# A chunked state-space scan kept in PSUM with one scan per tile, and a softmax whose rows are scaled on ScalarE

## The chip, the cores and the metric

The kernel runs on one core of one Trainium2 chip. The metric is the device time of one execution in microseconds (us). A profiled execution gives a trace of every engine: PE is the matrix engine (TensorE), DVE is VectorE, ACT is ScalarE, POOL is GpSimd, and SP is the engine whose queue issues the DMAs.

## The reference

Two layers (DEPTH = 2) of a gated mixer on x with 512 rows and width 1024, all in float32. Cut to what matters:

```
proj  = x @ w_in[l]         # u, z_ssm, c_q, c_kv, k_rope, z_mla, q_mem, z_mem, gate logits
y_ssm = S5(u)               # diagonal complex recurrence h[t] = lam * h[t-1] + B u[t];  y = Re(C h) + d * u
y_ssm = GLU(gelu(y_ssm)) * silu(z_ssm)
y_mla = causal attention, 8 heads, scores scaled by 96 ** -0.5, softmax over the row
y_mem = attention into 256 memory rows, 4 heads, scores scaled by 128 ** -0.5, softmax
x     = LayerNorm(ALPHA * x + (sum of gate * (branch @ p_branch)) @ w_out)
```

The S5 branch works on 512 features in 32 groups of 16, with 64 states a group. `gelu` is the tanh form.

## The kernel before

Every large matmul is three products of float32r parts (`mm3`, L72; lines 75, 76 and 77 in the trace), so an operand has to be split into a high part (a cast, mostly on ACT: L551, with a factor L554) and a low part (a subtraction, mostly on DVE: L552, with a factor L555) before PE can use it. `E.clk` counts the matmul time that the program has issued so far, in us of full-rate matmuls.

**Order of the work.** PE runs its instructions in the order in which the program writes them. The other engines and SP's DMA queue get an order from a scheduler, and each then works through its own list in that order: a waiting instruction holds up all that stand behind it on its engine. One layer is: the latents, then the memory keys (layer 0) and the memory attention (`mem_phase`), then one merge, two z tiles (`zs=2`), the GLU tiles (`glu_tile`, which reads the four entries of `E.g` in turn for k = 0 to 3), the latent attention (`mla_phase`) and the output.

**The S5 branch** is a background stream, `s5_stream` (L523). `tick` lets it go one stage on whenever `E.clk` has reached the value that the stream gave last. So its matmuls stand between those of the memory attention and the merge, at distances that a table of delays (`CFG`, L1282) gives in matmul time. A layer has four u tiles; `s5_tile` (L432) does one, of eight groups, in these stages:

- U is loaded (L443); `kp`: 16 small matmuls (L451, L452), copied to `kt` on ACT (L454), two small DVE operations (L458) and two DMAs to `kd` (L459);
- `tp`: two times four transposes (L465), each copied to `bmT` on ACT (L466);
- `tz` is loaded back from `kd` (L469); the next tile's operators are started on GpSimd (`s5_pool`, L358);
- `pb`: eight matmuls of 64 columns (L475), and then on DVE the chain L478 to L493: rotate (four operations), eight scans of 64 columns (L485), rotate back (four) into `z`;
- `py`: matmuls with `tz` and `U`, then with `t.cl` and `z` (L500); GELU on ACT and DVE (L501 to L505);
- `yt`: transposes (L509), a copy `y` on ACT (L511), a DMA out (`yd`, L513) and back (`yb`, L515), and the split of `yb` (L519, which calls `split_to`: L554 on ACT, L555 on DVE) into `E.g`.

`kp`, `tp`, `pb`, `py` and `yt` share one PSUM buffer (`s5=1`), so each can start only when the one before it has been read.

The softmax (`softmax_ops`, L713) takes the row maximum on DVE (L716), multiplies it by -scale on DVE (L717), takes exp on ACT (L718), inverts the sum on DVE (L719) and scales the row on DVE (L720); `mem_scores` calls it 32 times in the two layers and `mla_scores` 64 times.

Of the kernel before, what the change touches and what calls it, by code (L numbers as in the profile page):

```python
# [256 lines left out]
def param_setup(E):  # L257
    """The small S5 parameters of both layers."""
# [50 lines left out]
def rope_tables(E):  # L309
    """Cosines and signed sines of the rope angles, features on partitions."""  # L310
# [26 lines left out]
def s5_powers(E, l):  # L337
    """Powers of the discrete poles of one layer, then those of their phases."""
# [19 lines left out]
def s5_pool(E, l, ut):  # L358
    """Chunk operators of the eight groups of one u tile, as far as GpSimd builds them."""
# [61 lines left out]
def u_tile(E, l, ut):  # L421
    """One tile of u^T, regrouped through DRAM for the chunked scan."""
# [9 lines left out]
def s5_tile(E, l, ut, t):  # L432
    """Chunked scan of eight groups; leaves the split GELU of the SSM output in E.g.

    Yields how much matmul time should pass before its next stage."""
# [41 lines left out]
    a, b = mid("ra"), mid("rb")  # L477
# [69 lines left out]
def split_to(E, hi, lo, src, scale=1.0, eng=None):  # L547
    """hi + lo = scale * src, both float32r."""
# [22 lines left out]
def wblock(E, src, n=512, eng=None):  # L571
    """One [128, n] float32 block of weights as two float32r parts."""
# [26 lines left out]
def w_in_tile(E, l, t, eng=None):  # L599
    """One 128-column tile of x @ w_in, transposed, in PSUM."""  # L600
# [10 lines left out]
def warm_up(E):  # L611
    """Matmuls of zeros that open the tensor engine's clock gate while the first loads are under way."""
# [7 lines left out]
def first_tiles(E, l):  # L620
    """The latent tiles side by side, as x arrives."""
# [44 lines left out]
def gate2(E, ps):  # L666
    """2 * silu of a PSUM tile."""
# [7 lines left out]
def mem_load(E, tags):  # L675
    """mem^T, two feature tiles per block."""
# [61 lines left out]
def mem_values_out(E, l, h, Ps, z, fill):  # L738
    """Attention output of one memory head times its SiLU gate (twice)."""
# [19 lines left out]
def latents(E, l):  # L759
    """RMS-normalised q and kv latents (two parts each) and the rotated shared key."""  # L760
# [53 lines left out]
def scale_latents(E, l, cs, rs):  # L814
    """Norms and gains applied to the latents."""
# [12 lines left out]
def rotary_sums(E):  # L828
    """The partial sums of the shared key added up, as they are and with swapped halves."""
# [5 lines left out]
def rotate_key(E, ps):  # L835
    """The rotated shared key, two parts."""
# [9 lines left out]
def mla_v(E, l, i):  # L846
    """Values of four heads, two key tiles to a tile."""
# [13 lines left out]
def mla_k(E, l, hp):  # L861
    """Keys of two heads, with the rotated part."""
# [16 lines left out]
def mla_q(E, l, hp, j, wq):  # L879
    """Rotated queries of one head."""  # L880
# [11 lines left out]
    split_to(E, q[0][0:96, :], q[1][0:96, :], qf[0:96, :])  # L892
# [4 lines left out]
def mla_scores(E, q, k, Ps):  # L897
    """Softmax rows of one head, by query tiles."""
# [528 lines left out]
```

## Time and profile before

| | |
|---|---|
| three runs | 1161.16, 1162.88 (median), 1163.74 us |
| profiled execution | span 1161.9 us from the first to the last instruction, mean granted PE clock 0.965 |
| busy PE, DVE, ACT, POOL | 1075.1 (93%), 781.0 (67%), 456.9 (39%), 486.9 (42%) us |
| chain that ended last | PE 64%, DVE 20%, DMA 8% |

The profiled execution's own time lies in its span and the little around it, which no row shows; the median of the runs is 1.0 us above the span. A busy share of an engine is an average over the whole span. What an engine waited for is found in the table of waits, and where PE ran slowly in the tables by window, whose column PEclk is the granted clock as a share of full speed.

### The profile page before, as it was taken

The page shows a single profiled execution, that of the slowest core. Times are in us where ns is not written, and L with a number is a line of the kernel's source. Part 1 is how long each engine was busy: PE and PEld are TensorE (multiplying, and loading weights), DVE is VectorE, ACT ScalarE, POOL GpSimd, SP SyncE. Part 2 cuts the span into 40 slices and gives each one's busy share as a digit, 9 for nine tenths or more (in the row PEclk, how much of TensorE's full clock was granted, in tenths as well). Part 3 has the DMA queues.
Part 4 walks back from the last instruction along what each step waited for, and adds up shares of the span by engine and source line. Part 5 has one row for each costly group of instructions (what it writes and reads, how often), then busy time and mean ns, then how long its engine had stood idle before and what let it go on. Part 6 is the DMA issues. An engine that isn't in the chain of part 4 may idle for free.

```text
span 1161.9 us, 15913 instructions
## 1 busy us (share of the span) xinstructions
PE 1075.1 (93%) x5584; PEld 862.6 (74%) x5584; DVE 781.0 (67%) x1522; ACT 456.9 (39%) x906; POOL 486.9 (42%) x577
## 2 busy tenths in 40 slices
PE   9859897799999999999989979879999999999995
PEld 6658775677877777788868767667888777778885
DVE  7696969747687784753585796695547767644428
ACT  5314342233554443333334334323335544433331
POOL 3997854762023243763540365481000333320163
PEclk9969998999999999999989989989999999999998
DMA  6423242445222222444544424334332222234341
GB/s 212 146 65 122 55 114 69 108 106 126 89 80 66 67 64 66 135 127 128 155 133 139 116 64 114 76 85 118 104 100 82 71 66 65 73 110 126 102 144 73
DMA packets 87664, 117.96 MB, mean 102 GB/s; under 512 B 24096, under 2 KB 36512, under 8 KB 87584
## 3 DMA queue, kind: packets, MB, share of 16 engines
q1 hardware_dynamic: 86944, 114.85, 34.7%
q0 software_dynamic: 640, 2.10, 0.7%
q8 instruction: 44, 0.72, 0.3%
q14 instruction: 36, 0.29, 0.1%
HBM read 107.37 MB, written 9.55 MB: 101 GB/s over the span
## 4 chain that ended last, share of the span: by engine, by line
PE 64%; DVE 20%; DMA 8%; issue 4%; ACT 3%; POOL 1%; SPq 0%; DVEq 0%; ACTq 0%; POOLq 0%
PE mm L75 17%; PE mm L77 17%; PE mm L76 17%; DVE w L552 4%; PE av L929 2%; DVE rb L485 2%; DMA yb<-yd 2%; DMA raw<-in_w_mem_kv 2%; PE tp L921 2%; DMA yd<-ra 2%; PE py L500 1%; PE pb L475 1%; DVE P L720 1%; DVE hl L552 1%; DVE mx L716 1%
## 5 line engine op out<-in xcount | busy, mean ns | idle before, releaser
L75 PE MATMUL mm<-X,w 128*128 128x512 f32 x740 | 300.2, 406 | 0.2 <-ACT X L551 0.2
L77 PE MATMUL mm<-X,w 128*128 128x512 f32 x740 | 290.8, 393 | 0.0
L76 PE MATMUL mm<-X,w 128*128 128x512 f32 x740 | 290.1, 392 | 0.2 <-DVE X L552 0.2
L552 DVE TENSOR_TENSOR w<-raw,w 128x512 fp32r<-128x512 f32 (+2 forms) x247 | 211.8, 862 | 114.9 <-ACT w L551 113.9
L551 ACT CAST w<-raw 128x512 fp32r<-128x512 f32 (+1 forms) x317 | 191.9, 607 | 206.7 <-PE mm L77 71.9
L552 POOL TENSOR_TENSOR w<-raw,w 128x512 fp32r<-128x512 f32 x70 | 92.8, 1328 | 307.8 <-ACT w L551 123.5
L75 PEld LDWEIGHTS mm<-X,w 128*128 128x128 f32 x740 | 141.1, 191 | 30.6 <-issue 3.2
L77 PEld LDWEIGHTS mm<-X,w 128*128 128x128 f32 x740 | 139.6, 189 | 31.4 <-DVE w L552 0.8
L76 PEld LDWEIGHTS mm<-X,w 128*128 128x128 f32 x740 | 140.6, 190 | 26.7 <-DVE X L552 0.7
L77 PE MATMUL mm<-hl,w 128*128 128x512 f32 (+1 forms) x296 | 111.3, 376 | 15.5 <-DVE w L552 15.5
L75 PE MATMUL mm<-hl,w 128*128 128x512 f32 (+1 forms) x296 | 113.1, 382 | 0.0
L76 PE MATMUL mm<-hl,w 128*128 128x512 f32 (+1 forms) x296 | 110.6, 374 | 0.0
L77 PEld LDWEIGHTS mm<-hl,w 128*128 128x128 f32 x296 | 58.0, 196 | 25.8 <-DVE w L552 16.4
L75 PEld LDWEIGHTS mm<-hl,w 128*128 128x128 f32 x296 | 58.3, 197 | 8.9 <-issue 0.5
L76 PEld LDWEIGHTS mm<-hl,w 128*128 128x128 f32 x296 | 58.1, 196 | 8.6
L987 ACT ACTIVATE thg<-mm,bg 128x512 f32<-128x512 f32 x48 | 32.9, 686 | 63.3 <-PE mm L77 63.3
L872 POOL TENSOR_SCALAR hl<-hl 32x512 fp32r<-32x512 f32 x32 | 22.5, 702 | 74.1 <-PE mm L76 54.0
L718 ACT ACTIVATE P<-sa,mx 128x128 f32<-128x128 f32 (+1 forms) x64 | 33.8, 528 | 47.4 <-DVE mx L717 47.4
L998 POOL TENSOR_TENSOR macc<-macc,thg 128x512 f32<-128x512 f32 x16 | 24.4, 1526 | 65.3 <-DVE thg L997 61.6
L720 DVE TENSOR_SCALAR P<-P,mx 128x256 f32<-128x256 f32 (+2 forms) x96 | 47.3, 493 | 2.6
L997 DVE SCALAR_TENSOR_TENSOR thg<-thg,mm 128x512 f32<-128x512 f32 x32 | 22.0, 687 | 39.3 <-PE mm L77 39.2
L375 POOL MEMSET bt<- 128x16 f32 x8 | 0.9, 110 | 109.9 <-PE kp L452 109.9
(386 smaller groups left out, 2047.3 us busy)
## 6 DMA issues: line engine op xcount, KB each, us to landing
raw<-in_w_in SPq DMA_DIRECT2D x188, 256.0 KB
raw<-in_p SPq DMA_DIRECT2D x48, 256.0 KB
raw<-in_w_mem_kv SPq DMA_DIRECT2D x32, 256.0 KB
raw<-in_w_out SPq DMA_DIRECT2D x32, 256.0 KB
tz<-kd SPq DMA_DIRECT2D x8, 512.0 KB
raw<-in_w_glu SPq DMA_DIRECT2D x16, 256.0 KB
raw<-in_xT SPq DMA_DIRECT2D x8, 256.0 KB
raw<-in_memT SPq DMA_DIRECT2D x8, 256.0 KB
```

What stands on the lines that cost most here:

```text
L75: t.matmul(out, lhsT=a[0], rhs=b[0], start=start, stop=False)
L76: t.matmul(out, lhsT=a[0], rhs=b[1], start=False, stop=False)
L77: t.matmul(out, lhsT=a[1], rhs=b[0], start=False, stop=stop)
L485: v.tensor_tensor_scan(out=b[:, o], data0=E.r8[:, gi:gi + 1].to_broadcast([128, 64]), data1=a[:, o], initial=0.0, op0=ALU.mult, op1=ALU.add)
L551: nc.scalar.copy(hi, src)
L552: (eng or nc.vector).tensor_tensor(out=lo, in0=src, in1=fl(hi), op=ALU.subtract)
L718: nc.scalar.activation(out=P, in_=ps, func=AF.Exp, bias=mx[:, 1:2], scale=scale, accum_out=mx[:, 2:3])
L720: nc.vector.tensor_scalar(out=P, in0=P, scalar1=mx[:, 3:4], scalar2=None, op0=ALU.mult)
L921: nc.tensor.transpose(tp[:, cols(t)], Ps[t][:, cols(kb)], E.ident)
L929: mm = lambda out, rhs, start, stop: nc.tensor.matmul(out, lhsT=w, rhs=rhs, start=start, stop=stop)
L987: nc.scalar.activation(out=th, in_=pg, func=AF.Tanh, bias=E.bg2[:, col:col + 1], scale=0.5)
L998: (v if last else nc.gpsimd).tensor_tensor(out=E.macc[m], in0=E.macc[m], in1=th, op=ALU.add)
```

## The change

In the S5 tile the rotated input, the scanned values and the rotation back stay in `pb`, in PSUM; only the cross terms go to SBUF (`b`). One scan of 512 columns replaces eight of 64: its factors come from a new tile `r8`, which holds each group's pole radius 63 times behind a zero, so that the scan starts anew at each group. `r8` is filled by an ACT copy and a small memset. GELU loses one DVE operation, its factors going into the two ACT operations. The split of `yb` becomes a function `tail`, which runs in the next tile's `kp` stage (for the last tile after `tok_us`). The delays change. In the softmax the score scale goes into the split of the queries, the maximum comes out negated, and the row is scaled on ACT.

```diff
-def s5_tile(E, l, ut, t):
+def s5_tile(E, l, ut, t, tail):
...
-    yield 1.3
+    if tail is not None:
+        tail()
+    yield E.cfg["kt_us"]
...
-        yield 1.3 if h == 0 else E.cfg["pb_us"]
+        yield E.cfg["pb_us"]
...
+    r8 = mid("r8")
+    gi = l * NG + ut * 8
+    v.memset(g3(r8, 0, 1), 0.0)
+    nc.scalar.copy(g3(r8, 1, 63), E.r8[:, gi:gi + 8].rearrange("p (g o) -> p g o", o=1).to_broadcast([128, 8, 63]))
     pb = ptile("pb")
...
-    v.tensor_tensor(out=a, in0=pb, in1=t.cos, op=ALU.mult)
-    v.tensor_tensor(out=b[0:64, :], in0=pb[64:128, :], in1=t.sin[64:128, :], op=ALU.mult)
-    v.tensor_tensor(out=b[64:128, :], in0=pb[0:64, :], in1=t.sin[0:64, :], op=ALU.mult)
-    v.tensor_tensor(out=a, in0=a, in1=b, op=ALU.add)
-    for q in range(8):
-        o = slice(q * 64, q * 64 + 64)
-        gi = l * NG + ut * 8 + q
-        v.tensor_tensor_scan(out=b[:, o], data0=E.r8[:, gi:gi + 1].to_broadcast([128, 64]), data1=a[:, o], initial=0.0,
-                             op0=ALU.mult, op1=ALU.add)
...
-    v.tensor_tensor(out=g3(z, 1), in0=g3(b), in1=g3(t.cos), op=ALU.mult)
-    v.tensor_tensor(out=a[0:64, :], in0=b[64:128, :], in1=t.sin[64:128, :], op=ALU.mult)
-    v.tensor_tensor(out=a[64:128, :], in0=b[0:64, :], in1=t.sin[0:64, :], op=ALU.mult)
-    v.tensor_tensor(out=g3(z, 1), in0=g3(z, 1), in1=g3(a), op=ALU.subtract)
+    def swapped():
+        v.tensor_tensor(out=b[0:64, :], in0=pb[64:128, :], in1=t.sin[64:128, :], op=ALU.mult)
+        v.tensor_tensor(out=b[64:128, :], in0=pb[0:64, :], in1=t.sin[0:64, :], op=ALU.mult)
+
+    swapped()
+    v.tensor_tensor(out=pb, in0=pb, in1=t.cos, op=ALU.mult)
+    v.tensor_tensor(out=pb, in0=pb, in1=b, op=ALU.add)
+    v.tensor_tensor_scan(out=pb, data0=r8, data1=pb, initial=0.0, op0=ALU.mult, op1=ALU.add)
+    swapped()
+    v.tensor_tensor(out=pb, in0=pb, in1=t.cos, op=ALU.mult)
+    v.tensor_tensor(out=g3(z, 1, 63), in0=g3(pb, 0, 63), in1=g3(b, 0, 63), op=ALU.subtract)
...
-    nc.scalar.activation(out=a, in_=py, func=AF.Square)
-    v.tensor_scalar(out=a, in0=a, scalar1=0.044715, scalar2=1.0, op0=ALU.mult, op1=ALU.add)
-    v.scalar_tensor_tensor(out=a, in0=a, scalar=GELU_C, in1=py, op0=ALU.mult, op1=ALU.mult)
-    nc.scalar.activation(out=a, in_=a, func=AF.Tanh)
+    nc.scalar.activation(out=a, in_=py, func=AF.Square, scale=math.sqrt(0.044715))
+    v.scalar_tensor_tensor(out=a, in0=a, scalar=1.0, in1=py, op0=ALU.add, op1=ALU.mult)
+    nc.scalar.activation(out=a, in_=a, func=AF.Tanh, scale=GELU_C)
...
-    yield E.cfg["tok_us"]
-    h, lo = ftile2(E, "A")
-    w = lambda i: i.rearrange("p (n j) -> p j n", j=8)
-    split_to(E, w(h), w(lo), yb.rearrange("p (j n) -> p j n", j=8), 0.5)
-    E.g.append(HL(h, lo))
+
+    def tail():
+        h, lo = ftile2(E, "A")
...
+    return tail
...
-    nc.vector.reduce_max(out=mx[:, 0:1], in_=ps, axis=AX.X)
-    nc.vector.tensor_scalar(out=mx[:, 1:2], in0=mx[:, 0:1], scalar1=-scale, scalar2=None, op0=ALU.mult)
-    nc.scalar.activation(out=P, in_=ps, func=AF.Exp, bias=mx[:, 1:2], scale=scale, accum_out=mx[:, 2:3])
+    nc.vector.reduce_max(out=mx[:, 1:2], in_=ps, axis=AX.X, negate=True)
+    nc.scalar.activation(out=P, in_=ps, func=AF.Exp, bias=mx[:, 1:2], accum_out=mx[:, 2:3])
     nc.vector.reciprocal(out=mx[:, 3:4], in_=mx[:, 2:3])
-    nc.vector.tensor_scalar(out=P, in0=P, scalar1=mx[:, 3:4], scalar2=None, op0=ALU.mult)
+    nc.scalar.activation(out=P, in_=P, func=AF.Copy, scale=mx[:, 3:4])
...
-        q[h] = split(E, (yield from w_in_tile(E, l, Tiles.QM + h)))
+        q[h] = split(E, (yield from w_in_tile(E, l, Tiles.QM + h)), 128 ** -0.5)
...
-           mem_us=3.4, mla_us=2.5, lace_us=1.2, s5_first=(29.0, 0.0), s5_period=28.0, prio=400, tok_us=5.0,
-           pre_us=2.0, mem_lag=3, mla_lag=4, pb_us=1.3, py_us=9.0, gelu_us=4.5, zs=2, mv=range(6), warm=8, mk=(), sl=(0, 2, 4), tx=(0, 2, 5, 8))
+           mem_us=3.4, mla_us=2.5, lace_us=1.2, s5_first=(18.0, 0.0), s5_period=30.0, prio=400, tok_us=5.0,
+           pre_us=2.0, mem_lag=3, mla_lag=4, kt_us=3.0, pb_us=2.6, py_us=14.0, gelu_us=6.0, zs=2, mv=range(6), warm=8, mk=(), sl=(0, 2, 4), tx=(0, 2, 5, 8))
```

In `s5_stream` the new code passes each tile the `tail` of the tile before; in `mla_q` the split of the queries gets the factor 96 ** -0.5 in the same way.

What the edit does to the order shows in the lists of the engines. In program order a stage now stands as many us of matmuls later as its delay says. The first place is **PE where tile 0 of layer 0 ends** (`yt`) and tile 1 begins (`kp`); `mm` are tiles of the input projection, `bt`, `c0` and `cl` tile 1's operators. Before:

```order
L746 MATMUL tp_1546<-ident_75,P_1209 128x128 x2
L509 MATMUL yt_1555<-ident_75,rb_1325 128x128 [waits DVE_49,PE_49]
L509 MATMUL yt_1555<-ident_75,rb_1325 128x128 x3
L75 MATMUL mm_1453<-X_153,w_1516 128x512
L76 MATMUL mm_1453<-X_154,w_1516 128x512
```

Now:

```order
L77 MATMUL mm_1436<-X_153,w_1498 128x512
L513 MATMUL yt_1541<-ident_75,rb_1243 128x128 [waits PE_49]
L513 MATMUL yt_1541<-ident_75,rb_1243 128x128 x3
L451 MATMUL kp_1554<-c0_1202,bt_1192 32x16 [waits Activation_49,Pool_49]
L452 MATMUL kp_1554<-cl_1207,bt_1192 32x112 [waits Pool_49]
```

Between `yt` and the next `kp`, which need the same PSUM buffer, large matmuls stood before; now nothing does, and `kp` waits for ACT, which copies `yt` out. It is so between all tiles of a layer, six times in the two layers.

The second place is **ACT at the same hand-over**; `hl_1627` and `hl_1577` are the high parts of the split of tile 0's `yb`, `kt` and `bmT` are tile 1's copies, `P` rows of the softmax. Before:

```order
L511 COPY ra_1324<-yt_1555 128x512 [waits PE_49,Activation_49]
L718 ACTIVATE P_1523,mx_1536<-sm_1522,mx_1536 128x256 [waits DVE_49]
...
L551 CAST hl_1623<-tp_1618 128x512 [waits PE_49]
L554 ACTIVATE hl_1627<-yb_1563 128x8x64 [waits DMAHW2_49]
L551 CAST w_1834<-raw_1832 128x512 [waits DMAHW7_49,PE_49]
L718 ACTIVATE P_1594,mx_1607<-sm_1593,mx_1607 128x256 [waits DVE_49]
L454 COPY kt_1665<-kp_1648 128x256 [waits DMAHW0_49,PE_49,Pool_49]
...
L466 COPY bmT_1647<-tp_1690 128x512 [waits PE_49]
```

Now:

```order
L515 COPY r8_1231<-yt_1541 128x512 [waits PE_49]
L454 COPY kt_1571<-kp_1554 128x256 [waits PE_49,Pool_49]
...
L479 COPY r8_1745<-r8_407 128x8x63
L733 ACTIVATE P_1604,mx_1611<-sm_1603,mx_1611 128x256 [waits DVE_49]
L570 ACTIVATE hl_1577<-yb_1549 128x8x64 [waits DMAHW4_49]
...
L468 COPY bmT_1553<-tp_1635 128x512 [waits PE_49]
```

The split that waits for `yb` stood ahead of the next tile's `kt`; now it stands behind `kt` and ahead of the copies to `bmT`: of both in tile 1 of each layer, of the second one in the others.

The third place is **PE at the end of layer 0's S5**, after the last `yt`; `mm_2751` is the first GLU product, and its operands `hl_1577`, `hl_2065`, `hl_2425` and `hl_2747` are the four entries of `E.g` (before: `mm_2791`, and `hl_1627`, `hl_2070`, `hl_2424` and `hl_2757`). Before:

```order
L509 MATMUL yt_2708<-ident_75,rb_2538 128x128 [waits DVE_49,PE_49]
L509 MATMUL yt_2708<-ident_75,rb_2538 128x128 x3
L75 MATMUL mm_2699<-X_151,w_2702 128x512
...
L75 MATMUL mm_2791<-hl_1627,w_2794 128x512 [waits DVE_49,Activation_49]
...
L75 MATMUL mm_2791<-hl_2757,w_2794 128x512 [waits Activation_49]
```

Now:

```order
L513 MATMUL yt_2730<-ident_75,rb_2526 128x128 [waits DVE_49,PE_49]
L513 MATMUL yt_2730<-ident_75,rb_2526 128x128 x3
L75 MATMUL mm_2698<-X_153,w_2718 128x512
...
L75 MATMUL mm_2751<-hl_1577,w_2754 128x512 [waits Activation_49]
...
L77 MATMUL mm_2751<-hl_2425,w_2754 128x512
L75 MATMUL mm_2751<-hl_2747,w_2754 128x512 [waits Activation_49]
```

Three matmuls on `mm_2698` and nine on the first three entries stand between the last `yt` and the product that needs the split of this tile's `yb`; before, 45 matmuls stood between this `yt` and the first GLU product. At the end of layer 1, 27 matmuls (5.8 us of matmul time) stand there now.

On ACT, the copy into tile 0's `r8` (L479) stands in the setup, as the scheduler placed it: right after the cast of the weight block `w_645` and ahead of that of `w_656` and of the copy `ks`. It reads `E.r8`, whose last writer is GpSimd (L297). On SP, `yb` now stands behind the two `kd` DMAs of the next tile, which wait for the two DVE operations on `kt`; before, it stood ahead of them.

## Rows read from the trace of the kernel before

**Rows 1.** Windows of 100 us: length, busy us of each engine, PEclk, DMA share, GB/s.

```profile
300.00:400.00 100.00, 98.69 (x493) 77.86 (x492) 73.99 (x169) 51.94 (x117) 25.53 (x23) 1.00 0.25 73
...
700.00:800.00 100.00, 85.18 (x526) 69.66 (x525) 72.43 (x119) 35.32 (x70) 57.50 (x54) 0.91 0.38 97
```

**Rows 2.** Waits of PE: line waited for, us in total, times, longest us.

```profile
PE py L500 <- DVE z L493: 25.5, 4, 7.7
PE mm L77 <- DVE w L552: 15.5, 4, 10.3
PE tp L465 <- ACT kt L454: 9.1, 6, 2.5
PE av L76 <- DVE hl L552: 4.2, 1, 4.2
...
PE yt L509 <- DVE carve L110: 3.7, 1, 3.7
PE py L500 <- DVE mx L717: 2.9, 1, 2.9
```

**Rows 3.** Windows, PE alone: first and last of eight half-clock stretches, and their sum.

```profile
136.20:139.60 3.40, 3.40 (x22) 0.50 0.02 5
...
774.50:784.70 10.20, 5.00 (x32) 0.50 0.26 71
sum 40.80, PE 28.49; mean PE 3.56
```

**Rows 4.** Timeline of PE, layer 0, tile 1: start us, us, operation [idle before].

```profile
224.28 0.39 PE L76 MATMUL mm<-hl,w 128*128 128x512 f32 x1
224.50 0.39 PE L77 MATMUL mm<-hl,w 128*128 128x512 f32 x1
...
231.81 0.70 PE L500 MATMUL py<-cl,z 128*64 128x128 f32 x4 [6.55 <-DVE z L493]
```

**Rows 5.** Timeline of DVE in the same tile: the chain from pb to z.

```profile
214.63 0.69 DVE L478 TENSOR_TENSOR ra<-pb,cosn 128x512 f32<-128x512 f32 x1 [1.77 <-PE pb L475]
...
217.39 2.42 DVE L552 TENSOR_TENSOR w<-raw,w 128x512 fp32r<-128x512 f32 x1
219.73 5.46 DVE L485 TENSOR_TENSOR_SCAN rb<-r,ra 128x64 f32<-128x64 f32 x8
```

**Rows 6.** The chain by source line: count, ns min/median/max, first and last start.

```profile
L485 DVE TENSOR_TENSOR_SCAN rb<-r,ra x64: 257/265/1911, 122.9 to 813.5; 128x64 f32<-128x64 f32 x64
L478 DVE TENSOR_TENSOR ra<-pb,cosn x8: 679/691/693, 119.2 to 808.3; 128x512 f32<-128x512 f32 x8
L492 DVE TENSOR_TENSOR ra<-rb,sinn x8: 684/1492/1562, 131.0 to 815.2; 64x512 f32<-64x512 f32 x8
```

**Rows 7.** Timelines of ACT and SP behind yt, layer 0, tiles 0 and 2.

```profile
146.99 0.60 ACT L511 COPY ra<-yt 128x512 f32<-128x512 f32 x1
...
156.12 1.15 ACT L554 ACTIVATE hl<-yb 128x512 fp32r<-128x512 f32 x1 [3.71 <-DMA yb<-yd]
...
241.29 0.59 ACT L511 COPY ra<-yt 128x512 f32<-128x512 f32 x1 [0.45 <-PE yt L509]
...
242.86 0.61 SPq L513 DMA_DIRECT2D yd<-ra  x1
247.32 0.61 SPq L515 DMA_DIRECT2D yb<-yd  x1
...
251.89 1.15 ACT L554 ACTIVATE hl<-yb 128x512 fp32r<-128x512 f32 x1 [5.17 <-DMA yb<-yd]
```

**Rows 8.** Timelines of ACT, POOL and DVE in the setup.

```profile
39.81 0.62 ACT L551 CAST w<-raw 128x512 fp32r<-128x512 f32 x1 [2.28 <-DMA raw<-in_w_mem_kv]
...
48.04 0.74 POOL L297 TENSOR_TENSOR r<-r 128x64 f32<-128x64 f32 x1
...
64.50 14.30 DVE L552 TENSOR_TENSOR w<-raw,w 128x512 fp32r<-128x512 f32 x2
```

**Rows 9.** The scaling of the softmax rows by source line: count, ns min/median/max.

```profile
L720 DVE TENSOR_SCALAR P<-P,mx x96: 285/420/2031, 99.8 to 1021.8; 128x256 f32<-128x256 f32 x48, 128x128 f32<-128x128 f32 x16, 128x384 f32<-128x384 f32 x16, 128x512 f32<-128x512 f32 x16
```

More of the change, by code (lines that the diff above doesn't have):

```diff
@@ L472, in s5_tile @@
         E.s5t = s5_pool(E, l, ut + 1)
+    g3 = lambda x, a=0, n=64: x.rearrange("p (g n) -> p g n", g=8)[:, :, a:a + n]
+    r8 = mid("r8")
+    gi = l * NG + ut * 8
+    v.memset(g3(r8, 0, 1), 0.0)
+    nc.scalar.copy(g3(r8, 1, 63), E.r8[:, gi:gi + 8].rearrange("p (g o) -> p g o", o=1).to_broadcast([128, 8, 63]))
     pb = ptile("pb")
@@ L476, in s5_tile @@
                          start=True, stop=True)
-    a, b = mid("ra"), mid("rb")
-    v.tensor_tensor(out=a, in0=pb, in1=t.cos, op=ALU.mult)
-    v.tensor_tensor(out=b[0:64, :], in0=pb[64:128, :], in1=t.sin[64:128, :], op=ALU.mult)
-    v.tensor_tensor(out=b[64:128, :], in0=pb[0:64, :], in1=t.sin[0:64, :], op=ALU.mult)
-    v.tensor_tensor(out=a, in0=a, in1=b, op=ALU.add)
-    for q in range(8):
-        o = slice(q * 64, q * 64 + 64)
-        gi = l * NG + ut * 8 + q
-        v.tensor_tensor_scan(out=b[:, o], data0=E.r8[:, gi:gi + 1].to_broadcast([128, 64]), data1=a[:, o], initial=0.0,
-                             op0=ALU.mult, op1=ALU.add)
-    z = mid("z")
-    g3 = lambda x, o=0: x.rearrange("p (g n) -> p g n", g=8)[:, :, o:o + 63]
-    v.memset(z.rearrange("p (g n) -> p g n", g=8)[:, :, 0:1], 0.0)
-    v.tensor_tensor(out=g3(z, 1), in0=g3(b), in1=g3(t.cos), op=ALU.mult)
-    v.tensor_tensor(out=a[0:64, :], in0=b[64:128, :], in1=t.sin[64:128, :], op=ALU.mult)
-    v.tensor_tensor(out=a[64:128, :], in0=b[0:64, :], in1=t.sin[0:64, :], op=ALU.mult)
-    v.tensor_tensor(out=g3(z, 1), in0=g3(z, 1), in1=g3(a), op=ALU.subtract)
+    b, z = mid("rb"), mid("z")
+    v.memset(g3(z, 0, 1), 0.0)
+    def swapped():
[8 more added lines that the diff above has]
+    v.tensor_tensor(out=g3(z, 1, 63), in0=g3(pb, 0, 63), in1=g3(b, 0, 63), op=ALU.subtract)
     yield E.cfg["py_us"]
@@ L515, in s5_tile @@
     nc.sync.dma_start(out=yb.rearrange("p (i n) -> p i n", i=8), in_=yd.rearrange("c i g n -> g (c i) n"))
-    yield E.cfg["tok_us"]
-    h, lo = ftile2(E, "A")
-    w = lambda i: i.rearrange("p (n j) -> p j n", j=8)
-    split_to(E, w(h), w(lo), yb.rearrange("p (j n) -> p j n", j=8), 0.5)
-    E.g.append(HL(h, lo))
+    def tail():
+        h, lo = ftile2(E, "A")
+        w = lambda i: i.rearrange("p (n j) -> p j n", j=8)
+        split_to(E, w(h), w(lo), yb.rearrange("p (j n) -> p j n", j=8), 0.5)
+        E.g.append(HL(h, lo))
+    return tail
 def s5_stream(E, l, first, period):
     base = E.clk + first
+    tail = None
     for ut in range(4):
@@ L529, in s5_stream @@
         yield max(base + ut * period, E.clk)
-        for d in s5_tile(E, l, ut, t):
+        tile = s5_tile(E, l, ut, t, tail)
+        while True:
+            try:
+                d = next(tile)
+            except StopIteration as e:
+                tail = e.value
+                break
             yield E.clk + d
+    yield E.clk + E.cfg["tok_us"]
+    tail()
 class Tiles:
@@ L704, in mem_keys, with softmax_rows, softmax_ops @@
         E.km.append(split(E, ps))
-def softmax_rows(E, P, ps, scale):
+def softmax_rows(E, P, ps):
     with E.tc.high_priority(E.cfg["prio"]):
-        softmax_ops(E, P, ps, scale)
-def softmax_ops(E, P, ps, scale):
+        softmax_ops(E, P, ps)
+def softmax_ops(E, P, ps):
     nc = E.nc
     mx = E.sm.tile([128, 4], F32, name="mx", tag="mx", bufs=6)
-    nc.vector.reduce_max(out=mx[:, 0:1], in_=ps, axis=AX.X)
-    nc.vector.tensor_scalar(out=mx[:, 1:2], in0=mx[:, 0:1], scalar1=-scale, scalar2=None, op0=ALU.mult)
-    nc.scalar.activation(out=P, in_=ps, func=AF.Exp, bias=mx[:, 1:2], scale=scale, accum_out=mx[:, 2:3])
+    nc.vector.reduce_max(out=mx[:, 1:2], in_=ps, axis=AX.X, negate=True)
+    nc.scalar.activation(out=P, in_=ps, func=AF.Exp, bias=mx[:, 1:2], accum_out=mx[:, 2:3])
     nc.vector.reciprocal(out=mx[:, 3:4], in_=mx[:, 2:3])
-    nc.vector.tensor_scalar(out=P, in0=P, scalar1=mx[:, 3:4], scalar2=None, op0=ALU.mult)
+    nc.scalar.activation(out=P, in_=P, func=AF.Copy, scale=mx[:, 3:4])
 def mem_scores(E, h, q, Ps):
@@ L732, in mem_scores @@
             o = cols(b, 256)
-            softmax_rows(E, P[:, o], ps[:, o], 128 ** -0.5)
+            softmax_rows(E, P[:, o], ps[:, o])
         Ps.append(P)
@@ L891, in mla_q @@
     q = ftile2(E, "A")
-    split_to(E, q[0][0:96, :], q[1][0:96, :], qf[0:96, :])
+    split_to(E, q[0][0:96, :], q[1][0:96, :], qf[0:96, :], 96 ** -0.5)
     yield
@@ L906, in mla_scores @@
         P = E.pp.tile([128, 512], F32, name="P", tag="P")
-        softmax_rows(E, P[:, 0:n], ps[:, 0:n], 96 ** -0.5)
+        softmax_rows(E, P[:, 0:n], ps[:, 0:n])
         Ps.append(P)
```

1 line of the change is left out of this document (added).

## The prediction

> **What bounds the kernel now.** I read the windows first. In the attention stretches PE has hardly a gap at full clock: 98.69 of 100 us with PEclk 1.00, while DVE and ACT are far from full; where S5 runs it is busy 85.18 us at 0.91 [rows 1]. So PE sets the time, and what the change does to DVE and ACT counts only where PE waits for them. The waits of PE come next [rows 2]. Most of them are S5's: `py` for `z` 25.5 us in four waits, `py` behind a softmax maximum (the same late chain) 2.9, `tp` for the copy `kt` 9.1 in six, and two that stand beside the chain on DVE, `av` 4.2 and `yt` 3.7: **45.4 us**. The 15.5 us behind weight splits are setup, 10.3 of them one wait.
>
> [...] The timelines show the cause in layer 0's tile 1. On DVE the chain starts at 214.63; a weight split of 2.42 us and eight scans of 5.46 us are in it [rows 5]; PE, which had run its large matmuls every 0.22 us, sits idle for 6.55 us until 231.81 [rows 4], 17.2 us after the chain's start.
>
> **The change part by part, against the span of 1161.9 us** (the runs' median is 1.0 us above it).
>
> *The chain.* Eight operations of 0.69 us with an operand in PSUM (L478) [rows 6] and one scan of 512 columns, which no row shows. Its bounds are 0.69 us (an ordinary operation of that width) and 8 x 0.265 = 2.1 us (eight scans of 64, their starts included); I take 1.4, the middle. That makes 8 x 0.69 + 1.4 = 6.9 us. In DVE's new list up to four weight splits still stand inside the chain; at 0.7 us (an undisturbed operation) to 2.42 [rows 5] each they make it 9.7 to 16.6 us. In PE's new list some 67 large matmuls, 14.8 us at 0.22 [rows 4], lie between `pb` and `py`; before, `py_us` was 9. So `py` is in time but for the worst mixes, up to 1.8 us late: 0 to +8 x 1.8 = 14 us, and I take **+3**, near zero, since all four splits would have to be slow at once.
>
> The rows bear on one reason against working in place. A PSUM operand costs DVE nothing visible here: L478 takes 679 to 693 ns, the undisturbed L492, all in SBUF, 684 [rows 6]; and L478 has no slow cases, while the median of L492 is 1492. [...]
>
> *What goes.* With `kt_us` at 3.0 the copy to `kt`, which made `tp` wait, lies beside matmuls; with the scans gone, DVE is free for `av`; `yt` stands 1.5 us later and meets a shorter queue. All 45.4 us of gaps and 14.2 of half clock are at stake: **-59.6**.
>
> *`kp` straight behind `yt`.* PSUM is handed over only when ACT has copied `yt`: 0.45 us to its start and 0.59 [rows 7]. Six hand-overs: 6 x 1.0 = **+6** (bounds 5 and 9, if ACT is in a cast).
>
> *ACT behind `yb`.* From the end of the copy to the landing of `yb` it took 10.0 us in tile 2 and 8.5 in tile 0 [rows 7]; the high part takes 1.15, and the next copy to `bmT`, as wide as the copy of `yt`, 0.6. ACT works in order, so that copy ends 10.3 to 11.8 us after `kp` could begin. In tile 1 of layer 0 the second `tp` needs it after 36 matmuls, 8.1 us: 2.2 to 3.7 us late, 3.0 taken, and long enough for a half-clock stretch (14.2 / 8 = 1.8): 4.8. In tile 1 of layer 1 42 matmuls, 9.4 us: 1.6 late. In the four others only the second copy is behind `yb`, which `pb` needs after 10.7 us: 0 to 1.1, taken 0.4: 1.6. Sum **+8** (0 to 17).
>
> *The last `yb` of a layer.* High part ready 0.7 + 9.3 + 1.2 = 11.2 us after `yt`. In layer 0 PE has 3 + 9 matmuls until then, 2.7 us: a wait of 8.5, and 1.8 for the clock. In layer 1 27 + 9, 8.0 us: 3.2 and 1.8. Together **+15** (11 to 18). Before, 45 matmuls ahead of the GLU hid it.
>
> *The copy into `r8` in the setup.* The other seven find `E.r8` long written, but the first stands on ACT ahead of a weight cast that ran at 39.81, and reads what GpSimd finishes at 48.04 + 0.74 = 48.8 [rows 8]. PE would want that weight at about 43: some 6 us of waiting. Behind it comes PE's wait of 10.3 us [rows 2], whose releaser, two splits in 14.30 us [rows 8], does not depend on it and may swallow all; or the late casts meet the same slow splits. 0 to +11; **+5** taken.
>
> *Softmax.* 96 row scalings of 0.42 us median [rows 9] leave DVE for ACT, and 96 small operations go. They lie beside a full PE [rows 1]; ACT, at 51.94 of 100 us, has room. If that cover went, the transposes would wait for some 0.5 us a row. **0** (bounds -2 and +5). GELU's missing operation and the added factors in the query splits: 0, under the same matmuls.
>
> *Sum.* -59.6 + 3 + 6 + 8 + 15 + 5 = -22.6: a span of 1139.3, and with the 1.0 above it **1140 us**.
>
> **The rivals.**
>
> *Nearly the full gain.* ACT finds `yb` landed in time, the setup absorbs its 6 us and only `kp` (5) and the last `yb` without half clock (8.5 + 3.2 = 11.7) remain: -59.6 + 16.7 = -42.9, **1120 us**. For it speaks the 10.3 us gap behind the setup; against it the 8.5 us even of the fast landing.
>
> *The chain is still late.* If the DVE list with its splits, not the scans, sets `z`, or GpSimd's operators come later because tiles now follow each other closely, about half of the `py` waits stay, 14 us with 4 of half clock, less the 3 already counted: 1140 + 15 = **1155 us**. For it: 2.42 us for one split beside GpSimd [rows 5]; against it: 14.8 us of distance.
>
> *Slower: `yb` is queued late on SP.* `yb` now stands behind the two `kd` DMAs, and these behind two DVE operations on `kt` in a queue full of splits. Before, `yb` was issued 4.5 us after `yd` [rows 7], so the first 4 us cost nothing; every us beyond it moves `yb`, the split on ACT and the `bmT` copies, and PE waits in each of six tiles. The time before is reached when each of the six costs 23 / 6 = 3.8 us more than in my sum, half clock (1.8) included: a `kd` about 2 us too late. At 4 us too late, 6 x (4 + 1.8) = 35: 1140 + 35 = **1175 us**. Against it: the chain's scans, the largest block on DVE, are gone, and `kt` comes at a tile's start, where the chain before has ended.
>
> *The change doesn't pull.* PE's waits merely move (chain to hand-over), and the half clock stays: within 2 us of 1163. It needs +37 to grow to +58, which several terms' upper bounds would have to make up together.
>
> **How the numbers follow.** Forecast, 1133 to 1148: 0.50. Nearly full gain: 0.20. Chain late: 0.17. No pull: 0.05. Slower: 0.08. The range leaves out the slow rival and the far end: **1119 to 1158**. A measurement here tells 0.2%, about 2.3 us, from no change: faster 0.87, same 0.05, slower 0.08.
>
> **What would show it.** Right: the waits of `py` for `z` fall from 25.5 to under 5 us, `tp` for `kt` vanishes, and in their place stand `kp` for the copy of `yt` (about 1 us, six times), `tp` or `pb` for `bmT`, and one long wait of the first GLU product in layer 0 (8 to 9 us); the chain takes near 7 us of DVE's own time; half-clock stretches shrink from eight to three or four; the attention windows stay as they are. Wrong: `py` waits stay above 10 us (chain late), PE waits for `bmT` several us in all six tiles (slower), or the attention windows lose PE time to the scaling on ACT.

## The result

The changed kernel took 1143.09 us (median of four runs, 1139.53 to 1143.73) against 1162.02 for the kernel before: a ratio of 0.9842, 95% interval 0.9814 to 0.9871. The forecast was 1140, the range 1119 to 1158. The profiled execution has a span of 1140.6 us; the forecast's span was 1139.3.

The waits of PE, as in [rows 2], now read (line waited for, us in total, times, longest us). `sm` are the scores of the memory attention and `av` its product with the values; `hl L570` and `hl L571` are the high and the low part that a split with a factor makes, that of `yb` among them:

```profile
PE mm L77 <- DVE w L568: 13.0, 2, 12.0
PE mm L75 <- ACT hl L570: 10.5, 2, 7.5
PE kp L451 <- ACT r L515: 6.4, 6, 1.9
PE tx L1077 <- DVE mv L155: 4.2, 1, 4.2
PE tp L467 <- ACT bmT L468: 4.1, 2, 3.9
PE yt L513 <- DVE rb L509: 3.9, 1, 3.9
PE sm L77 <- DVE hl L571: 3.7, 2, 3.4
PE mm L75 <- ACT w L567: 3.6, 1, 3.6
```

Every wait of `py` for `z` (25.5 us) and of `tp` for `kt` (9.1) has gone. In their place stand the hand-overs: `kp` for the copy of `yt`, six times; the first GLU product for the last `yb` (hl L570), once in each layer; `tp` for `bmT`; and one that the forecast did not have, `sm` for a low part on DVE. The 13.0 us for `w` and the 3.6 us for `w L567` lie in the setup, before the first memory scores.

The half-clock stretches in the S5 parts, as in [rows 3], are five instead of eight, where three or four were forecast (first, last and sum; PE busy and PEclk):

```profile
152.70:159.50 6.80, 5.84 (x18) 0.50 0.56 147
...
828.50:835.30 6.80, 6.14 (x15) 0.50 0.29 78
sum 30.80, PE 23.89; mean PE 4.78
```

PE is busy for 23.89 us in them. In the third of them (282.4 to 289.2 us, PEclk 0.50) large matmuls started 0.43 us apart, and right behind it, at full clock, 0.23 us apart. So I take half of the busy time as their cost, an estimate: 11.9 us, against 28.49 / 2 = 14.2 by [rows 3]: fewer stretches, but fuller ones. The attention stretch was and is at full clock, the S5 stretch of layer 1 is fuller (compare [rows 1]):

```profile
300.00:400.00 100.00, 99.11 (x496) 77.74 (x495) 63.75 (x133) 61.94 (x139) 25.27 (x23) 1.00 0.25 74
...
700.00:800.00 100.00, 94.26 (x556) 77.25 (x555) 65.13 (x94) 40.09 (x75) 50.79 (x42) 0.98 0.41 106
```

The chain's operations, by source line (compare [rows 6]):

```profile
L492 DVE TENSOR_TENSOR pb<-pb,cosn x8: 679/696/700, 110.2 to 797.3; 128x512 f32<-128x512 f32 x8
```

```profile
L494 DVE TENSOR_TENSOR_SCAN pb<-r,pb x8: 1216/1222/1229, 112.1 to 798.8; 128x512 f32<-128x512 f32 x8
```

None of them has a slow case any more, and the one scan takes 1.22 us.

### The profile page after: what moved, and what is told of

It is laid out like the page before. It is cut to its first block, busy times and chain, and to the rows that moved or that the text cites. A ratio compares the mean times of both kernels' runs of the same rounds, so it can differ in the third digit from the quotient of the medians.

```text
span 1140.6 us, 15730 instructions
## 1 busy us (share of the span) xinstructions
PE 1069.4 (94%) x5584; PEld 856.6 (75%) x5584; DVE 692.1 (61%) x1274; ACT 508.1 (45%) x1010; POOL 485.5 (43%) x577
## 4 chain that ended last, share of the span: by engine, by line
PE 71%; DVE 11%; DMA 7%; issue 4%; ACT 3%; POOL 3%; SPq 0%; DVEq 0%; ACTq 0%; POOLq 0%
PE mm L75 19%; PE mm L77 19%; PE mm L76 19%; PE av L944 2%; PE tp L936 2%; DVE w L568 2%; DMA yb<-yd 2%; DMA yd<-r 1%; PE py L504 1%; DMA raw<-in_w_in 1%; PE pb L482 1%; DMA raw<-in_w_out 1%; DMA raw<-in_w_mem_kv 1%; DMA raw<-in_xT 1%; DVE hl L571 1%
## 5 line engine op out<-in xcount | busy, mean ns | idle before, releaser
L568 DVE TENSOR_TENSOR w<-raw,w 128x512 fp32r<-128x512 f32 (+2 forms) x247 | 204.5, 833 | 131.6 <-ACT w L567 130.4
L567 ACT CAST w<-raw 128x512 fp32r<-128x512 f32 (+1 forms) x317 | 191.7, 606 | 196.2 <-PE mm L77 73.8
L75 PE MATMUL mm<-hl,w 128*128 128x512 f32 (+1 forms) x296 | 113.5, 383 | 10.5 <-ACT hl L570 10.5
L735 ACT ACTIVATE P<-P,mx 128x256 f32<-128x256 f32 (+2 forms) x96 | 51.4, 543 | 16.8 <-DVE mx L734 16.5
L75 PE MATMUL mm<-w,hl 128*128 128x512 f32 (+1 forms) x88 | 34.9, 397 | 5.8 <-ACT w L567 3.6
```

What stands on the lines that cost most here:

```text
L567: nc.scalar.copy(hi, src)
L568: (eng or nc.vector).tensor_tensor(out=lo, in0=src, in1=fl(hi), op=ALU.subtract)
L735: nc.scalar.activation(out=P, in_=P, func=AF.Copy, scale=mx[:, 3:4])
```

## The experiments

Times are medians of four runs; ratios are against runs of the kernel before on the same chip, with 95% intervals.

**1. The new chain alone**, in the kernel before: `pb` in place and one scan, with old delays, old place of the split, old GELU and old softmax.

```diff
     pb = ptile("pb")
...
-    a, b = mid("ra"), mid("rb")
...
+    swapped()
+    v.tensor_tensor(out=pb, in0=pb, in1=t.cos, op=ALU.mult)
+    v.tensor_tensor(out=pb, in0=pb, in1=b, op=ALU.add)
+    v.tensor_tensor_scan(out=pb, data0=r8, data1=pb, initial=0.0, op0=ALU.mult, op1=ALU.add)
```

> The kernel before with the new chain alone (in place in PSUM, one scan; old delays, old place of the yb split, old GELU and softmax). My theory, that PE's waits at py are what the time hangs on: z comes some 10 us after pb instead of 16 to 18, py stands 10 to 12 us behind pb, so the py waits fall from 28.4 us (25.5 + 2.9) to about 4 and their half clock goes with them; the other S5 waits (tp for kt 9.1) stay, and none of the new hand-over waits arises: 1130 to 1140 us. Rival, that the new distances are what does it: z still comes after py in most tiles, 2 to 4 us each, py waits above 12 us: about 1150.

Measured: 1134.22 us, ratio 0.9772 (0.9747 to 0.9797): faster than the whole change. The waits of `py` by the table of waits:

```profile
PE tp L465 <- ACT kt L454: 12.3, 5, 4.1
...
PE py L503 <- issue: 3.6, 4, 1.8
...
PE py L503 <- DVE mx L720: 1.6, 1, 1.6
PE py L503 <- DVE z L495: 1.3, 2, 0.7
```

So the new chain takes the `py` waits from 28.4 to 6.5 us without the new distances. (Experiment 2 shows that the new distances end them too, with the old chain.) Part of the 27 us is not the chain's: of the profiled 31.6 us, 8.5 lie before the first memory scores (see the last section), and 23 behind them.

**2. The change with the old chain.**

```diff
-    v.tensor_tensor_scan(out=pb, data0=r8, data1=pb, initial=0.0, op0=ALU.mult, op1=ALU.add)
...
+    for q in range(8):
+        o = slice(q * 64, q * 64 + 64)
...
+        v.tensor_tensor_scan(out=b[:, o], data0=E.r8[:, gi:gi + 1].to_broadcast([128, 64]), data1=a[:, o], initial=0.0,
```

> The changed kernel with the old chain (operands in SBUF, eight scans) and all the rest new. My theory: the old chain takes 16 to 18 us from pb to z and the new distance is 14.8 to 18.8, so py waits come back in part of the tiles, 0 to 3 us each: 1144 to 1156 us, with py waits of 5 to 15 us. Rival, that the delays alone bring the gain: py waits under 3 us and 1140 to 1143.

Measured: 1156.02 us, ratio 0.9960 (0.9926 to 0.9993). The time is the one that my theory gave, its mechanism is not: no wait of `py` is in the table at all. PE waits for splits instead, on DVE and on ACT:

```profile
PE mm L77 <- DVE w L565: 18.4, 5, 10.4
PE mm L75 <- ACT hl L567: 12.8, 2, 7.2
PE sm L77 <- DVE hl L568: 7.5, 4, 5.0
```

Of the 18.4 us, 16.3 lie in the setup, where no chain has run (13.0 in the change). What is new stands in the S5 parts: `sm` 3.8 us more than in the change, `av` 3.5, the GLU 2.3, a split of weights 1.7, and seven half-clock stretches instead of five (PE busy for 34.28 us in them, against 23.89). The distance of 14.8 us does cover even the old chain; what the old chain costs is paid by other work.

**3. The softmax alone**, in the kernel before.

```diff
-    nc.vector.tensor_scalar(out=P, in0=P, scalar1=mx[:, 3:4], scalar2=None, op0=ALU.mult)
+    nc.scalar.activation(out=P, in_=P, func=AF.Copy, scale=mx[:, 3:4])
```

> The kernel before with the new softmax alone (scale in the queries, negated maximum, rows scaled on ACT). My theory: it works beside a full PE, and only the memory attention beside S5 could feel the freer DVE: within 3 us of before, 1158 to 1165. Rival, that the freer DVE brings a good part of the gain: 1152 or less, with the py waits under 20 us.

Measured: 1156.26 us, ratio 0.9958 (0.9932 to 0.9983): a gain of some 5 us where I had said none, though not the rival's 10. Most of it lies where softmax and S5 share DVE: the table of waits has no `py` wait for a softmax maximum any more (2.9 us in [rows 2]), and those for `z` are 2.6 us less:

```profile
PE py L500 <- DVE z L493: 22.9, 6, 6.6
```

**4. One scan, but the operands in SBUF**, in the changed kernel.

```diff
-    v.tensor_tensor(out=pb, in0=pb, in1=t.cos, op=ALU.mult)
-    v.tensor_tensor(out=pb, in0=pb, in1=b, op=ALU.add)
-    v.tensor_tensor_scan(out=pb, data0=r8, data1=pb, initial=0.0, op0=ALU.mult, op1=ALU.add)
+    v.tensor_tensor(out=a, in0=a, in1=b, op=ALU.add)
+    v.tensor_tensor_scan(out=b, data0=r8, data1=a, initial=0.0, op0=ALU.mult, op1=ALU.add)
```

> The changed kernel with one scan of 512 columns but the chain's operands in SBUF as before. My theory, that the chain's length matters only against the distance to py: four operations with both inputs in SBUF stretch from 0.7 to some 1.5 us beside GpSimd, z comes about 3 us later, still inside 14.8 us: within 3 us of the changed kernel, py waits under 4 us. Rival, that the PSUM operands are what frees the chain: py waits above 6 us and 1149 or more.

Measured: 1157.47 us, ratio 0.9974 (0.9938 to 1.0011): 14 us more than the change, and no different from eight scans in SBUF (experiment 2). The rival's time, but again without a wait of `py`. Operations with both inputs in SBUF are stretched, one of them in six tiles of eight, by source line:

```profile
L493 DVE TENSOR_TENSOR ra<-rb,sinn x8: 687/1476/1509, 120.0 to 820.0; 64x512 f32<-64x512 f32 x8
```

and PE waits more for DVE's other work, by the table of waits:

```profile
PE mm L77 <- DVE w L564: 17.7, 4, 12.2
...
PE sm L77 <- DVE hl L567: 7.2, 3, 3.4
...
PE av L76 <- DVE hl L564: 3.9, 2, 2.7
```

Those three were 13.0, 3.7 and 0.2 us in the changed kernel. Of the first, 13.3 us lie in the setup, and 4.2 in layer 1's S5, where the change has none. Seven half-clock stretches in the S5 parts instead of five (PE busy for 31.71 us in them, against 23.89) make up some 4 us more. (The profiled execution is the longest of the four, its span 19.7 us above the change's.) How the chain reaches other work shows in layer 0's tile 0, on DVE's timeline. Here:

```profile
111.58 0.69 DVE L486 TENSOR_TENSOR ra<-pb,cosn 128x512 f32<-128x512 f32 x1 [0.40 <-PE pb L482]
...
118.51 1.47 DVE L492 TENSOR_TENSOR ra<-rb,sinn 64x512 f32<-64x512 f32 x1
120.00 1.45 DVE L493 TENSOR_TENSOR ra<-rb,sinn 64x512 f32<-64x512 f32 x1
...
121.56 0.67 DVE L567 SCALAR_TENSOR_TENSOR hl<-mm,hl 128x512 fp32r<-128x512 f32 x1
```

In the change:

```profile
108.70 0.69 DVE L488 TENSOR_TENSOR rb<-pb,sinn 64x512 f32<-64x512 f32 x1 [0.40 <-PE pb L482]
...
115.53 0.68 DVE L489 TENSOR_TENSOR rb<-pb,sinn 64x512 f32<-64x512 f32 x1
116.25 0.69 DVE L571 SCALAR_TENSOR_TENSOR hl<-mm,hl 128x512 fp32r<-128x512 f32 x1
```

The low part `hl` that `sm` needs comes 10.0 us after the chain's start instead of 7.6, and PE waits 1.8 us for it, where it did not wait in the change. Some 1.9 us are stretched operations of the chain; the rest is one operation more of the chain ahead of `hl`, in a list that the scheduler has made anew. The two causes were not separated.

**5. Layer 0's S5 ten us earlier**: `s5_first=(8.0, 0.0)` in the changed kernel.

```diff
-s5_first=(18.0, 0.0)
+s5_first=(8.0, 0.0)
```

> The changed kernel with layer 0's S5 started 10 us of matmul time earlier (s5_first 8 instead of 18). My theory: the last yt of layer 0 then stands some 10 us farther ahead of the first GLU product, its wait of 7.5 us falls to 0 to 1 and the half-clock stretch behind it goes: 8 to 10 us less, 1131 to 1136. Rival: the setup (GpSimd's operators, DVE's splits) cannot feed an earlier first tile, the waits appear there instead: 1140 or more.

Measured: 1137.09 us, ratio 0.9767 (0.9738 to 0.9796), 6 us less than the change and 1 above what I gave. The long GLU wait of layer 0 is gone (that of 4.1 us is layer 1's), but GpSimd's operators now come late for `kp`, three times:

```profile
PE mm L75 <- ACT hl L570: 4.9, 2, 4.1
...
PE kp L452 <- POOL cl L403: 3.0, 3, 1.7
```

So the wait in the last-`yb` term is shown, and so is a part of the rival. A half-clock stretch of 3.4 us still stands behind the GLU's start (275.5 to 278.9 us), and the waits of `sm` for DVE's low part rose from 3.7 to 5.0 us.

**6. The split of `yb` behind the chain** instead of in the `kp` stage.

```diff
-    if tail is not None:
-        tail()
     yield E.cfg["kt_us"]
...
+    if tail is not None:
+        tail()
     yield E.cfg["py_us"]
```

> The changed kernel with the split of yb issued behind pb and its chain instead of in the kp stage. My theory, that ACT standing at yb delays the copies to bmT: the tp wait for bmT (3.9 us in tile 1 of layer 0) and the half-clock stretch behind it go, about 5 us less: 1136 to 1140. Rival, that the wait is only moved to what stands behind the split now: within 2 us of the changed kernel, 1141 to 1145.

Measured: 1134.85 us, ratio 0.9751 (0.9727 to 0.9774), 8 us less than the change. The waits of `tp` for `bmT` are gone and, beyond what I had expected, those of `sm` for DVE's low part fell from 3.7 to 0.4 us. The hand-overs of `kp` (6.4 us) and of the GLU (10.7) stay as they were. Two waits of `av` for DVE, 3.4 us, are new. ACT and DVE both stood at `yb`, and both held back what PE needed.

**7. All delays and the place of the split as before**; new chain, GELU and softmax.

```diff
-s5_first=(18.0, 0.0), s5_period=30.0
+s5_first=(29.0, 0.0), s5_period=28.0
...
-kt_us=3.0, pb_us=2.6, py_us=14.0, gelu_us=6.0
+kt_us=1.3, pb_us=1.3, py_us=9.0, gelu_us=4.5
```

> The changed kernel with the delays and the place of the yb split of the kernel before: new chain, GELU and softmax stay. My theory from the runs so far (the chain alone gave 27 us, the softmax alone 5): the two add up, 1126 to 1132 us; the new delays and the later split then cost 11 to 17 us. Rival, that the delays are needed once the rest is new: 1140 or more.

Measured: 1123.53 us, ratio 0.9660 (0.9635 to 0.9686), below even the sum of experiments 1 and 3 (GELU's missing DVE operation is in it too). **The moved stages cost the change some 20 us.** No wait of `kp`, none of the GLU is left; the largest in the S5 parts is now:

```profile
PE tp L465 <- ACT kt L454: 12.7, 5, 4.3
```

**8. The same, with one delay of the change kept**: 3.0 us between `kp` and `tp`.

```diff
-kt_us=1.3
+kt_us=3.0
```

> As the run with the old delays, but with 3.0 instead of 1.3 us between kp and tp, the only one of the new delays kept. My theory: the waits of tp for the copy kt (12.3 us in five waits with the chain alone) and their half clock go: 8 to 14 us below the run with all old delays. Rival: tp then waits for something else that is as late (the split of yb on ACT, the operators of GpSimd): within 4 us of it.

Measured: **1116.71 us, ratio 0.9600 (0.9569 to 0.9630)**, the fastest of all, ahead of both kernels. That is 6.8 us less than experiment 7: less than the 8 to 14 of my theory, more than the rival's 4. The `tp` waits for `kt` are gone, but `py` waits 4.3 us where it waited 1.6, and `tp` 2.4 us for `bmT`. What S5 still costs PE is small:

```profile
PE yt L511 <- DVE carve L110: 4.6, 1, 4.6
PE py L502 <- issue: 4.3, 3, 2.3
...
PE tp L465 <- ACT bmT L466: 2.4, 2, 2.0
```

and one half-clock stretch is left in both S5 parts (183.1 to 186.5 us):

```profile
183.10:186.50 3.40, 3.05 (x10) 0.50 0.40 108
```

**9. Eight scans, in PSUM**, in the changed kernel (without the copy into `r8`).

```diff
-    v.tensor_tensor_scan(out=pb, data0=r8, data1=pb, initial=0.0, op0=ALU.mult, op1=ALU.add)
+    for q in range(8):
+        o = slice(q * 64, q * 64 + 64)
+        v.tensor_tensor_scan(out=pb[:, o], data0=E.r8[:, gi + q:gi + q + 1].to_broadcast([128, 64]), data1=pb[:, o], initial=0.0,
```

> The changed kernel with the chain in place in PSUM but eight scans of 64 columns instead of one of 512 (no copy into r8 either). The runs so far gave 1156 for SBUF and eight scans and 1157 for SBUF and one scan, against 1143 for PSUM and one scan. My theory now: it is the PSUM operands that count, since a scan that reads PSUM does not stand behind GpSimd; eight of them take about 8 x 0.27 = 2.1 us instead of 1.2: 1141 to 1147. Rival, that merging the scans counts once the chain is in PSUM: 1150 or more, with waits of PE for DVE's splits as with SBUF.

Measured: 1143.72 us, ratio 0.9853 (0.9802 to 0.9904): the change's time. With experiments 2 and 4 this makes a square: SBUF and eight scans 1156, SBUF and one 1157, PSUM and eight 1144, PSUM and one 1143. Where the operands lie is worth some 13 us; the number of scans makes no difference that these runs could tell (the interval of this one is 12 us wide).

**10. The first copy into `r8` on GpSimd.**

```diff
-    nc.scalar.copy(g3(r8, 1, 63), E.r8[:, gi:gi + 8].rearrange("p (g o) -> p g o", o=1).to_broadcast([128, 8, 63]))
+    (nc.gpsimd.tensor_copy if l == 0 and ut == 0 else nc.scalar.copy)(g3(r8, 1, 63), E.r8[:, gi:gi + 8].rearrange("p (g o) -> p g o", o=1).to_broadcast([128, 8, 63]))
```

> The changed kernel with the first of the copies into r8 on GpSimd instead of ACT. My forecast put that copy's stand on ACT in the setup at 5 us, between 0 and 11. If it costs that, PE reaches the first memory scores 3 to 6 us earlier and the time is 1137 to 1140; if the wait of 12 us behind it swallows it, as the trace of the changed kernel suggests: within 2 us of 1143, with the 3.6 us gap near 42 us gone and the later gap as long or longer.

Measured: 1143.97 us, ratio 0.9844 (0.9796 to 0.9892): no difference, within an interval of 5.6 us to either side. PE reaches the first memory scores at 96.2 us, not earlier than in the change (93.8). The wait for the cast shrinks, those for the slow splits grow:

```profile
PE mm L77 <- DVE w L568: 16.3, 5, 11.1
...
PE mm L75 <- ACT w L567: 1.8, 1, 1.8
```

Their sum was 13.0 + 3.6 = 16.6 us in the change and is 18.1 here.

**11. Experiment 8 with `py` 1.5 us later.**

```diff
-py_us=9.0
+py_us=10.5
```

> As the run with the old delays and 3.0 us between kp and tp, with py_us 10.5 instead of 9. The waits of py there (4.3 us in three, put down to issue) end within 0.1 us of z; my theory is that py waits for the PSUM buffer, which the chain now holds to its end. Moved 1.5 us back, they vanish: 3 to 5 us less, 1111 to 1115. Rival, that they move to yt or the GLU: 1116 to 1118.

Measured: 1131.73 us, ratio 0.9755 (0.9722 to 0.9788): **15 us more** than experiment 8, a miss of both theories. The waits of `py` did go; the hand-over came back. With `yt` later and the period as it was, the next `kp` comes 0.5 to 1.6 us sooner behind `yt` at five hand-overs of six, and at four of six the split that waits for `yb` runs on ACT between `kt` and `bmT`, where it did so at one before:

```profile
PE tp L465 <- ACT bmT L466: 6.8, 4, 3.6
PE yt L511 <- DVE carve L142: 4.2, 1, 4.2
...
PE tp L465 <- ACT kt L454: 4.1, 2, 2.5
PE mm L75 <- ACT hl L557: 3.1, 1, 3.1
```

In the S5 parts PE's waits are some 7.5 us longer than in experiment 8, and four half-clock stretches (PE busy for 16.11 us) instead of one (3.05) cost some 6.5 more.

**12. The same, GELU's two DVE operations at the softmax's priority.**

```diff
+    with E.tc.high_priority(E.cfg["prio"]):
+        v.scalar_tensor_tensor(out=a, in0=a, scalar=1.0, in1=py, op0=ALU.add, op1=ALU.mult)
```

> As the run before, with GELU's two DVE operations at the priority of the softmax. My theory: the yt wait of 4.6 us in layer 0, GELU behind the rope table's small operations on DVE, and its half-clock stretch of 3.4 us go: 5 to 6 us less than without, 1106 to 1110. Rival, that the rope table is then late itself or other DVE work waits: within 2 us of it.

Measured: 1124.66 us, ratio 0.9699 (0.9651 to 0.9748): 7 us less than experiment 11, as expected in size, though the two intervals meet and one of the four runs took 1131.76. The `yt` wait fell from 4.2 to 2.8 us only, while the `tp` waits for `bmT` and `kt` fell too, from 10.9 to 7.5 together. My reading, that GELU earlier means `yt` and `yb` earlier, was not tested by itself. On top of experiment 8, without the later `py`, it was not tried.

## Why the prediction was right, and where not

The sum came out at the right time: the span was 1.3 us off. So near a hit is partly luck, as the terms show. The terms, each against the trace of the changed kernel:

- *What goes* (-59.6). Of the 45.4 us of gaps, 41.3 went. The step "`yt` stands 1.5 us later and meets a shorter queue" failed: the wait of layer 0's `yt` is 3.9 us still, for GELU behind the rope table's small operations, and with the half clock behind it (4.33 us busy) it costs 3.9 + 2.2 = 6.1. No run shows the 14.2 us of half clock in this term, nor the 1.8 us a stretch in two terms below, as such: they halve the time that PE was busy at PEclk 0.50. The runs show that time, 28.49 us in eight stretches before and 23.89 in five now, and matmuls 0.43 us apart in one of them instead of 0.23; the PE wait at each stretch was 2.5 to 7.7 us before and 3.0 to 7.5 now.
- *The chain* (+3 for late `py`): 0. The scan takes 1.22 us, I had taken 1.4. But the reason that I gave for the chain's worth, its length against the distance to `py`, holds for the old distances (experiment 1) and was wrong for the new ones: experiments 2 and 4 have no `py` wait either and still lose 13 us. In the change the operations on PSUM are not held (none of the 72 took over 21 ns more than the shortest of its line), and DVE's other work comes sooner; that this carries all of the 13 us is argued from the waits and from one tile's timeline. The row was there, the spread of L492 against that of L478 [rows 6]; I used it against the cost of PSUM and not for its worth.
- *`kp` behind `yt`* (+6): 6.4.
- *ACT behind `yb`* (+8): 4.1 of gaps and 5.84 / 2 = 2.9 of clock, 7.0. The same cause on DVE, whose low part of `yb` also stands ahead of what PE needs, was not in my list: `sm` 3.7 and 1.7 of clock. Together 12.4. Experiment 6, which ends nearly all of both, took 8 us off the time, with 3.4 us of new waits.
- *The last `yb`* (+15): 10.5 of gaps, and 5.1 of clock ((4.08 + 6.14) / 2): 15.6. ACT's and PE's timelines at the end of layer 0:

```profile
274.52 0.59 ACT L515 COPY r<-yt 128x512 f32<-128x512 f32 x1 [1.81 <-PE yt L513]
...
283.62 1.12 ACT L570 ACTIVATE hl<-yb 128x512 fp32r<-128x512 f32 x1 [7.28 <-DMA yb<-yd]
```

```profile
284.79 0.79 PE L75 MATMUL mm<-hl,w 128*128 128x512 f32 x1 [7.53 <-ACT hl L570]
```

- *The copy into `r8`* (+5): nothing, at the low end of its range. ACT stood at it for 8.4 us, PE waited 3.6, but it reached the first memory scores at 93.8 us, against 96.3 in the kernel before: PE was busy for 8.25 us at half clock in the setup instead of 14.49. Experiment 10 moves the time by less than its interval.
- *Softmax* (0): about -5 when done alone (experiment 3), by DVE's relief beside S5. What it takes away there are mostly waits of `py`, which the -59.6 already count, so it is no further term of the sum. That cover ("a full PE") is true of the attention of the latents, where PE was busy for 99.11 of 100 us; it is not of the memory attention, which shares DVE with S5.

So the chain (3 us), `r8` (5) and the setup (2.5) came out shorter than the sum, the wait of `yt` (6.1) and the low part of `yb` (5.4) longer, and they met: that is the luck. The rivals: "nearly the full gain" and "the chain is still late" did not come. The "slower" one had the right place, the hand-over of `yb`, but not on SP: `yb` was issued 4.1 to 4.9 us behind `yd` in every tile, against 4.1 to 4.7 before.

What the forecast did not ask is whether the moved stages are worth having. Experiments 7 and 8 answer: the chain, GELU and the softmax give about 39 us with the old delays and 46 with `kt_us` alone, and the change's other delays and its later split give back 20 and 26 of them. Which of `pb_us`, `py_us`, `gelu_us` and the period does how much of that was not separated; the split's place is 8 us of it by experiment 6. The 6 us of experiment 5 are none of it, for the old delays start layer 0's S5 later, not earlier.

Why the old `py_us` of 9 is enough is seen in experiment 8's timeline of PE. `z` was ready at 253.00 us, when DVE's last operation of the chain ended, and `py` starts as a whole, its `tz` part too, at once behind it:

```profile
252.32 0.68 DVE L495 TENSOR_TENSOR z<-pb,rb 128x504 f32<-128x504 f32 x1
253.10 0.44 PE L502 MATMUL py<-tz,U 128*64 128x128 f32 x4 [2.31 <-issue]
```

The chain in place holds the PSUM buffer that `py` needs until its last operation; that this is why the wait shows no releaser in the table is my reading. Before, only the second part of `py` waited for `z`.

## What to carry to other kernels

When work on a shared engine is made cheaper, first run it alone, without the new spacing: here the spacing lost about half of what the cheaper work had won. In an in-order kernel a stage's distance has two ends: moving `py` away from its producer moved `yt` and `yb` onto the next tile's first copies, and 1.5 us decided over 15 us of time. And an operation's worth may lie in what queues behind it: a DVE chain with no wait of its own cost 13 us, and the waits that grew were mostly for splits of other work.

## What the runs showed of the hardware

- **Where DVE's operands lie.** With an operand in PSUM the chain's operations other than the scan took 669 to 700 ns in every case; none of the 72 operations of the changed kernel's chain, the scan included, was stretched, and 29 of them ran beside a GpSimd operation. In experiment 4, 18 of the 48 operations with both inputs in SBUF took over 60 ns more than the shortest of their line, by up to 0.9 us each and some 11 us in all; the worst line had a median of 1476 ns, three others 672 to 692. All 18 ran beside a GpSimd operation, and of the 30 others 24 ran beside none. No run here stopped GpSimd, so that it is what stretches them was not shown by itself.
- **DVE behind a run of GpSimd operations.** In the setup GpSimd runs ten operations of 1.0 to 1.9 us back to back, 12.7 us in all from 65.09 us, and one DVE split stood through all of them in the changed kernel (timeline of DVE):

```profile
65.20 13.17 DVE L568 TENSOR_TENSOR hl<-c,hl 128x512 fp32r<-128x512 f32 x1
```

In experiment 1 the two took turns instead: the same ten GpSimd operations took 16.5 us, and DVE's splits between them 1.2 to 2.4 us each:

```profile
72.80 2.41 DVE L555 TENSOR_TENSOR w<-raw,w 128x512 fp32r<-128x512 f32 x1
...
75.74 2.41 DVE L555 TENSOR_TENSOR w<-raw,w 128x512 fp32r<-128x512 f32 x2
```

PE's wait there was 3.6 us in two instead of 10.3 [rows 2] or 12.0 in one; this is most of the 8.5 us by which experiment 1 reached the memory scores earlier. What decides between the two was not found.
- **The scan's price.** In SBUF 64 columns take 265 ns [rows 6] and 512 take 1224 (median in experiment 4): (1224 - 265) / 448 = 2.1 ns a column. In PSUM it is 294 ns (median in experiment 9) and 1222 (median in the changed kernel): (1222 - 294) / 448 = 2.1 ns a column as well.
